# Three of four down batches in seven products, one operand sum made in DRAM by DMA, and activation sums three steps later, in a two-layer hybrid trunk

## The chip, the cores and the metric

The kernel runs on one core of one Trainium2 chip. The metric is device time in microseconds (us): the kernel before takes 2304.21 us, the median of three runs (2303.27 to 2304.63). All arithmetic that matters is fp32, done on TensorE as three products of split operands (below).

## The reference

Two layers over a sequence of 256 tokens and a width of 2048. Each layer is a mixer, a squared-ReLU MLP with a hidden width of 8192, and a gated embedding. Layer 0 mixes with differential attention, layer 1 with a gated recurrence.

```
for i in range(DEPTH):                       # DEPTH = 2
    xn = rmsnorm(h, g_mix[i])
    mix = diff_attention(...) if i % 2 == 0 else rglru_block(...)
    h = h + mix
    h = h + sqrelu_mlp(rmsnorm(h, g_mlp[i]), w_up[i], w_down[i])
    ple_gate = sigmoid(rmsnorm(h, g_ple[i]) @ w_ple_gate[i])
    h = h + ple_gate * (p[i] @ w_ple_proj[i])

def sqrelu_mlp(xn, w_up, w_down):            # w_up 2048x8192, w_down 8192x2048
    return square(relu(xn @ w_up)) @ w_down

def diff_attention(xn, w_qkv, ...):          # first of the program
    q, k, v = split(xn @ w_qkv); q = rmsnorm(q, g_q); k = rmsnorm(k, g_k); ...
```

## The kernel before, in words

Weights are streamed once from DRAM. SyncE's queue loads chunks of four 128-row tiles by 512 columns (1 MB) into a few raw buffers. `stream` walks over groups (one block of output columns each) and their steps; a step (`Sub`) is two weight tiles, 128x1024. For each step ScalarE writes a rounded copy `hi` (a cast) and VectorE the remainder `lo = raw - hi`; this pair of instructions is called a split here. TensorE then does three products for each pair of tiles: x_hi w_hi, x_lo w_hi, x_hi w_lo. Splits are written three steps ahead of the products, into four buffers in the attention part and six in the MLP.

The order of the work: the text is written step by step, `defer(n, ...)` puts a piece n steps later, and the framework's scheduler then lays out each engine's queue by its own estimate, letting an instruction go ahead of others on its engine when what it depends on is there. Each queue is then fixed, and an engine runs it strictly in order.

The q and k groups (eight, the first of the program): at the end of a group `qk_evict` takes 8 sums of squares (`q_ss`, VectorE), GpSimd makes `q_m` and `q_r` from them (`rstd`, L366 and L368), VectorE multiplies by `q_r` (L591) and goes on with the splits of the next group, which stand behind it in its queue.

The MLP: `up` groups (512 hidden columns each, 8 steps of 16 products) alternate with `down` groups. Two up groups make two batches of 512 hidden rows; a down group then multiplies up to four batches by 1024 of the 2048 output columns (one half). In a batch the product is a 2x2 block product; it is done plainly in 8 block products (4 steps of 12 matmuls), or by the Winograd form in 7 (7 steps of 6 matmuls). For a batch in seven, VectorE also makes sums of activation blocks (L810 to L815, at the end of the up group) and four sums of weight blocks (`split_form`, L470: U1 = W11 + W12, T2 = U1 + W22, T3 = W12 + W22, T4 = T2 + W21), and splits seven operands instead of four. Before the change, every second batch is in seven. `middle` and `evict` of `down` join the products and add them to the residual `h`.

The pool for 128x1024 sums and for the activation sums is `t4`, three buffers.

Of the kernel before, what the change touches and what calls it, by code (L numbers as in the profile page):

```python
# [9 lines left out]
F32 = mybir.dt.float32  # L10
# [51 lines left out]
class Group:  # L62
# [41 lines left out]
class Blocks:  # L104


    def __init__(self, w, b, n0):
        r0 = b * BT * P
        rows = w[r0 : r0 + BT * P].rearrange("(c p) n -> p c n", p=P)
        self.chunks = [Chunk(rows[:, :, n0 + i * NB : n0 + (i + 1) * NB], BT) for i in range(2)]  # L110
        for c in self.chunks:
            c.ring = 1
        self.sums = {}

    def of(self, name):
        if name in self.sums:
            return self.sums[name]
        return self.chunks[int(name[2]) - 1].raw[:, int(name[1]) - 1 :: 2]


class SevenGroup:
# [4 lines left out]
    def __init__(self, w, batches, n0, hid, middle, evict):  # L126
        self.hid, self.middle, self.evict, self.subs, self.pre = hid, middle, evict, [], {}
        self.what = []
        for b, seven in batches:
            bl = Blocks(w, b, n0)  # L130
            if seven:
                for i, (form, _, _) in enumerate(FORMS):
# [9 lines left out]
        self.first, self.last = {}, {}  # L142
        for i, (_, form, nj) in enumerate(self.what):
# [3 lines left out]
        self.mid = max(self.last[k] for k in ("P1", "P5", "P6", "P7"))  # L147
# [27 lines left out]
def trunk_kernel(ctx: ExitStack, tc, a, out):  # L175
# [24 lines left out]
    sm = ctx.enter_context(tc.tile_pool(name="sm", bufs=4))  # L200
    ps_acc = ctx.enter_context(tc.tile_pool(name="ps_acc", bufs=6, space=PSUM))
# [189 lines left out]
    class Norm(Wide):  # L391
# [35 lines left out]
        def feed(self, nb):  # L427
            self.stat(nb)
            for b in range(2):
                defer(1 + b, lambda b=b: self.transpose(nb, b))  # L430


    def stream(groups):
# [38 lines left out]

        def split_to(i):
            while done["split"] < min(i + 1, len(subs)):
# [22 lines left out]
        for g in groups:  # L497
# [6 lines left out]
            for i, s in enumerate(g.subs):  # L504
# [7 lines left out]
                if seven:  # L512
                    prods = g.products(i, s)
                    for q in prods:
                        if q[0] not in acc:
                            acc[q[0]] = ps_tp.tile([P, NB], F32, name="tp") if q[0] in ("P3", "Z") else psum([P, NB])
# [5 lines left out]
                    if i == g.mid:  # L522
                        g.middle(acc)
# [24 lines left out]
                run_due()  # L548
            g.evict(acc)
# [223 lines left out]
    SLOTS = 4  # L773

    def is_seven(b):
        return b % 2 == 0

    def mlp(l, norm_in, norm_out):
# [3 lines left out]
        def batch(b):  # L782

            if not is_seven(b):
                both = big([P, 2, 2, 4, P], F32R)
                return Batch(False, both[:, 0], both[:, 1])
            if "x" not in space:
                space["x"] = x32([P, 2, 2, 2, 7, P])
            both = space["x"][:, b % SLOTS // 2]
            return Batch(True, both[:, 0], both[:, 1])  # L790

        def up_evict(b):


            def evict(acc):
                hid[b] = bt = batch(b)
                for j in range(2):
# [3 lines left out]
                    for i in range(2):  # L801
# [4 lines left out]
                        nc.vector.tensor_tensor(halves[i], two(ps[:, :SEQ]), two(other), op=ALU.add)  # L806
                    nc.scalar.activation(x, x, AF.Relu)
# [18 lines left out]
        def down(half, bs):  # L826
# [3 lines left out]
            keep = {}  # L830

            def middle(acc):
                c1, cb = t4([P, 2, NB]), t4([P, 2, NB])
                keep["P1"], keep["M"], keep["B"], keep["N"] = c1[:, 0], c1[:, 1], cb[:, 0], cb[:, 1]
                nc.scalar.copy(keep["P1"], acc["P1"])
                nc.vector.tensor_tensor(keep["M"], keep["P1"], acc["P6"], op=ALU.subtract)
                nc.vector.tensor_tensor(keep["B"], acc["P7"], keep["M"], op=ALU.add)
                for k, o in (("M", "M"), ("N", "B")):
                    nc.vector.scalar_tensor_tensor(
                        keep[k], in0=acc["P5"], scalar=-1.0, in1=keep[o], op0=ALU.mult, op1=ALU.subtract  # L840
                    )

            def evict(acc):
                r2 = norm_in().r2
                for t, n, ps, other in ((0, 0, "P2", "P1"), (1, 0, "P4", "B"), (0, 1, "P3", "M"), (1, 1, "Z", "N")):
                    hb = h[:, t, hs[n]]
                    for part in (acc[ps], keep[other]):
                        nc.vector.scalar_tensor_tensor(
                            hb, in0=part, scalar=r2[:, t : t + 1], in1=hb, op0=ALU.mult, op1=ALU.add
                        )  # L850
# [4 lines left out]
            groups.append(SevenGroup(a["w_down"][l], [(b, is_seven(b)) for b in bs], n0, hid, middle, evict))  # L855

        for b in range(0, NBT, 2):
            up(b)
            up(b + 1)
            down(int(b % 4 == 0), range(max(b - 2, 0), b + 2))  # L860
        down(1, range(NBT - 2, NBT))


    def ple(l, norm_in, norm_out):
# [13 lines left out]
        def gate_evict(nb):  # L878
            def evict(acc):
# [5 lines left out]
                if nb == 3 and l == 0:  # L885
                    defer(8, lambda: p_setup(1))
# [248 lines left out]
    defer(40, lambda: p_setup(0))  # L1135
# [31 lines left out]
```

## Time and profile before

| | us |
|---|---|
| median of three runs | 2304.21 |
| the profiled execution: its own time | 2303.79 |
| its span, first to last instruction | 2301.9 |
| TensorE busy in the span | 2277.8 (99%) |
| VectorE busy | 1709.6 (74%) |
| ScalarE busy | 1355.5 (59%) |
| GpSimd busy | 47.3 (2%) |

432 MB come in by SyncE's queue, which keeps the 16 DMA engines busy for 55.5% of the span. The profiled execution stands 0.42 us under the median. Around its span lie 1.9 us. A matmul's shown duration is longer than its share of time, since matmuls overlap; the distance from one start to the next is what it costs. The same holds, less strongly, for VectorE's long instructions.

### The profile page before, as it was taken

What the parts mean: (1) busy time and instruction counts of PE and PEld (TensorE: products, weight loads), DVE (VectorE), ACT (ScalarE), POOL (GpSimd) and SP (SyncE); (2) the same over time, 40 slices, a digit from 0 to 9 for tenths busy, and PEclk for the clock granted to TensorE, in tenths of its full rate; (3) what the DMA queues carried; (4) which work ended last, traced back from release to release, by engine and by line L of the source; (5) the groups of instructions that cost most, each with busy time, mean ns of one, the idle gap of its engine ahead of it and who ended that gap; (6) DMA issues with size and microseconds to landing.
All of it is one profiled execution on the core that took longest, in us unless ns stands there. A gap on an engine that the chain in (4) does not pass through costs nothing. (4 is left out here: it accounts for less than half of the span.)

```text
span 2301.9 us, 29004 instructions
## 1 busy us (share of the span) xinstructions
PE 2277.8 (99%) x11275; PEld 1913.4 (83%) x11275; DVE 1709.6 (74%) x2048; ACT 1355.5 (59%) x1836; POOL 47.3 (2%) x79
## 2 busy tenths in 40 slices
PE   8999999999999999999999999999999999999999
PEld 7888888888888888887888887888888888888787
DVE  6676655778878868879666767568887887887974
ACT  6555555655655645646557887555564564564653
POOL 2100000000000000000000000000000000000000
PEclk9999999999999999999999999999999999999999
DMA  7455556456547547545555565645745645745464
GB/s 244 165 185 168 165 171 214 168 182 237 181 162 242 187 161 244 175 162 186 193 190 190 165 201 173 202 157 200 256 151 179 238 167 181 239 167 179 174 210 146
DMA packets 221050, 434.80 MB, mean 189 GB/s; under 512 B 7326, under 2 KB 12064, under 8 KB 220912
## 3 DMA queue, kind: packets, MB, share of 16 engines
q1 hardware_dynamic: 220256, 432.04, 55.5%
q8 instruction: 88, 1.44, 0.3%
q0 software_dynamic: 608, 0.89, 0.2%
q14 instruction: 50, 0.41, 0.1%
q10 hardware_dynamic: 48, 0.02, 0.0%
HBM read 430.82 MB, written 2.10 MB: 188 GB/s over the span
## 5 line engine op out<-in xcount | busy, mean ns | idle before, releaser
L357 DVE TENSOR_TENSOR w_lo<-w_raw,w_hi 128x1024 fp32r<-128x1024 f32 x465 | 564.2, 1221 | 304.5 <-ACT w_hi L356 304.4
L356 ACT CAST w_hi<-w_raw 128x1024 fp32r<-128x1024 f32 x465 | 486.6, 1051 | 419.4 <-PE acc L352 214.9
L537 PE MATMUL acc<-x,w_hi 128*128 128x512 f32 x1368 | 477.3, 396 | 0.0
L350 PE MATMUL acc<-w_hi,x 128*128 128x512 f32 x1152 | 457.1, 397 | 0.0
L351 PE MATMUL acc<-w_lo,x 128*128 128x512 f32 x1152 | 450.4, 391 | 1.9 <-DVE w_lo L357 1.9
L352 PE MATMUL acc<-w_hi,x 128*128 128x512 f32 x1152 | 450.6, 391 | 0.0
L537 PE MATMUL acc<-x,w_lo 128*128 128x256 f32 x1368 | 368.5, 279 | 0.0
L537 PEld LDWEIGHTS acc<-x,w_hi 128*128 128x128 f32 x1368 | 251.9, 188 | 54.7
L537 PEld LDWEIGHTS acc<-x,w_lo 128*128 128x128 f32 x1368 | 257.8, 188 | 7.4
L352 PEld LDWEIGHTS acc<-w_hi,x 128*128 128x128 f32 x1152 | 216.7, 188 | 46.7 <-DVE x L357 0.2
L351 PEld LDWEIGHTS acc<-w_lo,x 128*128 128x128 f32 x1152 | 217.2, 189 | 44.9 <-DVE w_lo L357 3.1
L350 PEld LDWEIGHTS acc<-w_hi,x 128*128 128x128 f32 x1152 | 216.8, 188 | 41.7
L464 ACT CAST w_hi<-t 128x1024 fp32r<-128x1024 f32 x85 | 89.2, 1051 | 128.8 <-PE acc L537 73.9
L537 PE MATMUL acc<-x,big 128*128 128x512 f32 (+1 forms) x688 | 127.7, 338 | 0.0
L356 ACT CAST w_hi<-big 128x1024 fp32r<-128x1024 f32 x87 | 90.7, 1050 | 62.6 <-PE acc L537 26.7
L471 DVE TENSOR_TENSOR w_lo<-t,w_hi 128x1024 fp32r<-128x1024 f32 x85 | 103.8, 1222 | 30.3 <-ACT w_hi L464 30.1
L537 PE MATMUL acc<-x,v 128*128 128x512 f32 (+1 forms) x672 | 124.8, 338 | 0.0
L537 PEld LDWEIGHTS acc<-x,big 128*128 128x128 f32 x688 | 107.9, 188 | 15.5
L537 PEld LDWEIGHTS acc<-x,v 128*128 128x128 f32 x672 | 105.9, 188 | 15.0
L357 DVE TENSOR_TENSOR w_lo<-big,w_hi 128x1024 fp32r<-128x1024 f32 x87 | 105.3, 1218 | 14.1 <-ACT w_hi L356 14.1
L471 DVE TENSOR_TENSOR w_lo<-w_raw,w_hi 128x1024 fp32r<-128x1024 f32 x64 | 78.0, 1219 | 31.9 <-ACT w_hi L464 31.9
L518 PE MATMUL acc<-w_hi,x 128*128 128x512 f32 x256 | 100.3, 392 | 1.4 <-ACT w_hi L464 1.3
(277 smaller groups left out, 3570.0 us busy)
## 6 DMA issues: line engine op xcount, KB each, us to landing
w_raw<-in_w_up_dram SPq DMA_DIRECT2D x96, 1024.0 KB, 5.5
w_raw<-in_w_down_dram SPq DMA_DIRECT2D x96, 1024.0 KB, 5.2
w_raw<-in_w_qkv_dram SPq DMA_DIRECT2D x47, 1024.0 KB, 5.1
big<-in_w_up_dram SPq DMA_DIRECT2D x32, 1024.0 KB, 5.6
big<-in_w_down_dram SPq DMA_DIRECT2D x32, 1024.0 KB, 7.3
w_raw<-in_w_ple_gate_dram SPq DMA_DIRECT2D x32, 1024.0 KB, 5.2
w_raw<-in_w_in_rec_dram SPq DMA_DIRECT2D x32, 1024.0 KB, 5.4
w_raw<-in_w_o_attn_dram SPq DMA_DIRECT2D x16, 1024.0 KB, 5.1
```

The lines of the kernel that those rows point to most:

```text
L350: nc.tensor.matmul(ps, lhsT=lh, rhs=rh, start=start, stop=False)
L351: nc.tensor.matmul(ps, lhsT=lh, rhs=rl, start=False, stop=False)
L352: nc.tensor.matmul(ps, lhsT=ll, rhs=rh, start=False, stop=stop)
L356: nc.scalar.copy(hi, src)
L357: nc.vector.tensor_tensor(lo, src, hi.bitcast(F32), op=ALU.subtract)
L464: nc.scalar.copy(s.hi, src)
L471: nc.vector.tensor_tensor(s.lo, src, s.hi.bitcast(F32), op=ALU.subtract)
L518: nc.tensor.matmul(acc[k], lhsT=lh, rhs=rh, start=first, stop=False)
L537: nc.tensor.matmul(o, lhsT=lh, rhs=rh, start=k == 0 and n == 0, stop=k == g.nk - 1 and n == 1)
```

## The change

1. `is_seven` becomes `b % 4 != 1`: of 16 batches of a half, 12 are in seven products and 4 plain (before 8 and 8). `batch` gets other buffers for this.
2. The seven operands come in another order (W11, W21, W22, U1, T2, T3, T4), and three sums are left on VectorE. The fourth, U1 = W11 + W12, is made in DRAM: `Blocks.prepare` copies 512 KB of W12 to a scratch tensor and adds 512 KB of W11 to it, by two DMAs of GpSimd's queue, the second an accumulating one that waits for the first. SyncE later loads the scratch tensor in place of W12. `prepare` is written into the steps of the two up groups ahead of the down group that uses it (`g.pre`).
3. The ReLU, the square and the activation sums of a batch come three steps after the end of its up group (`defer(3, finish)`).
4. The joining of the products (`done`) is done as each product's last step is past, not in the middle and at the end.
5. Two pieces of small work move: the transposes of the norm behind the MLP (`feed`) come later, and the preparation of `p` (`p_setup`) moves into the last down groups.

The sixth split buffer of the MLP is put into memory left over (`spare`, `wx`).

```
-    ("W11", X11, "P1"), ("U1", S1, "P5"), ("T2", S2, "P6"), ("T3", S3, "P7"), ("W21", X12, "P2"),
-    ("T4", X22, "P4"), ("W22", S4, "P3"),
+    ("W11", X11, "P1"), ("W21", X12, "P2"), ("W22", S4, "P3"), ("U1", S1, "P5"), ("T2", S2, "P6"),
+    ("T3", S3, "P7"), ("T4", X22, "P4"),
 )
-SUMS = {"U1": ("W11", "W12"), "T2": ("U1", "W22"), "T4": ("T2", "W21"), "T3": ("W12", "W22")}
+SUMS = {"T2": ("U1", "W22", ALU.add), "T3": ("T2", "W11", ALU.subtract), "T4": ("T2", "W21", ALU.add)}
...
+    def prepare(self, nc, scratch):
+
+        nc.gpsimd.dma_start(scratch, self.cols[1][:, 0::2])
+        nc.gpsimd.dma_start(scratch, self.cols[0][:, 0::2], accum_op=ALU.add)
+        dst, _ = self.chunks[1].pieces[0]
+        self.chunks[1].pieces[0] = (dst, scratch)
...
+    scratch = ctx.enter_context(tc.tile_pool(name="scratch", bufs=10, space=bass.MemoryType.DRAM))
...
             if after in SUMS:
-                load_to(cidx[id(bl.chunks[1])])
-                one, two = (bl.of(nm) for nm in SUMS[after])
+                one, two, op = SUMS[after]
                 bl.sums[after] = t4([P, SK, NB])
-                nc.vector.tensor_tensor(bl.sums[after], one, two, op=ALU.add)
+                nc.vector.tensor_tensor(bl.sums[after], bl.of(one), bl.of(two), op=op)
...
-                    if i == g.mid:
-                        g.middle(acc)
+                    for k in acc:
+                        if g.last[k] == i:
+                            g.done(k, acc)
...
     def is_seven(b):
-        return b % 2 == 0
+        return b % SLOTS != 1
...
+                    fs.append((j, f, x))
+
+                def finish():
+                    for e in fs:
+                        form(*e)
+
+                defer(3, finish)
...
-                        norm_out().feed(2 * half + n)
+                        norm_out().feed(2 * half + n, 2 + 2 * n if half else 4 + 3 * n)
+                    if half == 0:
+                        defer(7, lambda: p_setup(l))
...
+            todo = [bl for g in groups[at + 2 :] for bl in g.sevens]
+            for i, bl in enumerate(todo):
+                g = groups[at + i % 2]
+
+                def prepare(_, bl=bl):
+                    bl.prepare(nc, scratch.tile([P, SK, NB], F32, name="u1"))
+
+                g.pre[1 + 2 * (i // 2)] = prepare
```

How the change moves instructions, at the two places that matter.

First, GpSimd's queue in the q and k part, at the start of the program. Before the change, between `q_m` (L366) and `q_r` (L368) of a group and those of the next stands nothing, or one small load:

```order
L366 TENSOR_SCALAR q_m<-q_ss 128x8 [waits DVE_49]
L300 DMA t_426<-in_lam_k_dram 128x128 [waits DMASW5_49]
L368 TENSOR_TENSOR q_r<-q_m,mhalf 128x8 [waits Pool_49]
L366 TENSOR_SCALAR q_m<-q_ss 128x8 [waits DVE_49]
L368 TENSOR_TENSOR q_r<-q_m,mhalf 128x8 [waits Pool_49]
L366 TENSOR_SCALAR q_m<-q_ss 128x8 [waits DVE_49]
L368 TENSOR_TENSOR q_r<-q_m,mhalf 128x8 [waits Pool_49]
L366 TENSOR_SCALAR q_m<-q_ss 128x8 [waits DVE_49]
L368 TENSOR_TENSOR q_r<-q_m,mhalf 128x8 [waits Pool_49]
```

After the change the same queue, from the second `q_m` on (now L383, with `q_r` at L385; L124 is the copy of a block of W12 to a scratch tensor `u`, L125 the accumulating DMA onto it; DMASW are the counters of GpSimd's own DMAs):

```order
L383 TENSOR_SCALAR q_m<-q_ss 128x8 [waits DVE_49]
L124 DMA u_7188<-in_w_down_dram 256x1x512 [waits DMASW4_49]
L385 TENSOR_TENSOR q_r<-q_m,mhalf 128x8 [waits Pool_49]
L124 DMA u_7738<-in_w_down_dram 256x1x512 [waits DMASW5_49]
L124 DMA u_7783<-in_w_down_dram 256x1x512
L125 DMA u_7188<-in_w_down_dram 256x1x512 [waits DMASW4_49]
L125 DMA u_7738<-in_w_down_dram 256x1x512 [waits DMASW5_49]
L125 DMA u_7783<-in_w_down_dram 256x1x512 [waits DMASW6_49,DMASW1_49]
L124 DMA u_7929<-in_w_down_dram 256x1x512 [waits DMASW2_49]
L124 DMA u_8472<-in_w_down_dram 256x1x512 [waits DMASW3_49]
L124 DMA u_8517<-in_w_down_dram 256x1x512
L125 DMA u_7929<-in_w_down_dram 256x1x512 [waits DMASW2_49]
```

Eight more DMAs follow before the third `q_m`; before the change nothing stood between. All 96 DMAs of `prepare`, of both layers, stand in GpSimd's queue ahead of the seventh and eighth `q_m`: 16 ahead of the first `q_m` and, between one `q_m` and the next, 14, 18, 14, 17, 14 and 3. None stands in the MLP's part of the queue. The scratch tensors are 48 different ones, so that no copy waits for a reader.

Second, VectorE's queue at the end of the second up group of a pair (batches 6 and 7 of layer 0) and the start of the down group. Before (L806 joins the halves of the up products, L471 and L357 are splits, of a batch in seven and of a plain one; the 128x512 rows are batch 7's activations):

```order
L471 TENSOR_TENSOR w_lo_5802<-t4_5782,w_hi_5801 128x1024
L471 TENSOR_TENSOR w_lo_5849<-t4_5804,w_hi_5848 128x1024
L471 TENSOR_TENSOR w_lo_5862<-w_raw_5734,w_hi_5861 128x1024
L806 TENSOR_TENSOR t2_5824<-acc_5647,t1_5825 128x2x128
L806 TENSOR_TENSOR t2_5824<-acc_5648,t1_5828 128x256
L806 TENSOR_TENSOR t2_5835<-acc_5649,t1_5836 128x2x128
L806 TENSOR_TENSOR t2_5835<-acc_5650,t1_5839 128x256
L471 TENSOR_TENSOR w_lo_5875<-t4_5864,w_hi_5874 128x1024
L357 TENSOR_TENSOR big_5823<-t2_5824,big_5823 128x512
L357 TENSOR_TENSOR big_5823<-t2_5835,big_5823 128x512
L471 TENSOR_TENSOR v4_5886<-w_raw_5759,v4_5885 128x1024
```

After, at the same place (L833 joins the halves, L486 is a sum of weight blocks, L487 a split of a batch in seven, L846 to L851 the activation sums):

```order
L487 TENSOR_TENSOR w_lo_5895<-w_raw_5834,w_hi_5894 128x1024
L833 TENSOR_TENSOR t4_5878<-acc_5687,t1_5879 128x2x128
L833 TENSOR_TENSOR t4_5878<-acc_5688,t1_5882 128x256
L833 TENSOR_TENSOR t4_5885<-acc_5689,t1_5886 128x2x128
L486 TENSOR_TENSOR t4_5897<-w_raw_5834 128x1024
L833 TENSOR_TENSOR t4_5885<-acc_5690,t1_5889 128x256
L846 TENSOR_TENSOR t4_5878<-t4_5878 128x256
L850 TENSOR_TENSOR t4_5878<-t4_5878 128x128
L851 TENSOR_TENSOR t4_5878<-t4_5878 128x128
L487 TENSOR_TENSOR w_lo_5908<-t4_5897,w_hi_5907 128x1024
L374 TENSOR_TENSOR big_5877<-t4_5878,big_5876 128x896
L846 TENSOR_TENSOR t4_5885<-t4_5885 128x256
```

Before, five of the seven operands' splits and all four sums stand ahead of the join; after, four splits and no sum, and batch 7, now in seven too, puts six activation sums and two larger splits between the rest. In TensorE's queue the products of the plain batch are drawn forward between those of T3 and T4.

## Rows read from the trace of the kernel before

**Rows 1.** The page, part 1: busy time, share of the span, instructions.

```profile
PE 2277.8 (99%) x11275; PEld 1913.4 (83%) x11275; DVE 1709.6 (74%) x2048; ACT 1355.5 (59%) x1836; POOL 47.3 (2%) x79
```

**Rows 2.** Waits: engine, line, waited for: us in total, times, longest.

```profile
POOL q_m L366 <- DVE q_ss L586: 133.6, 7, 25.6
...
DVE t L591 <- POOL q_r L368: 14.7, 8, 2.0
...
PEld acc L518 <- ACT big L464: 7.3, 5, 1.8
```

**Rows 3.** Timeline of TensorE: start, us, instruction; last attention and first seven-product steps.

```profile
399.72 0.39 PE L350 MATMUL acc<-w_hi,x 128*128 128x512 f32 x1
...
402.44 0.86 PE L537 MATMUL acc<-x,big 128*128 128x512 f32 x4
...
448.08 0.40 PE L518 MATMUL acc<-w_hi,x 128*128 128x512 f32 x1
...
449.46 0.40 PE L518 MATMUL acc<-v,x 128*128 128x512 f32 x1
...
450.87 0.40 PE L518 MATMUL acc<-big,x 128*128 128x512 f32 x1
```

**Rows 4.** Windows of two up groups and their down group (busy us, clock, DMA).

```profile
468.67:513.66 44.99, 44.99 (x258) 39.15 (x256) 33.18 (x40) 22.08 (x29) 0.00 (x0) 1.00 0.43 145
513.66:554.68 41.02, 41.02 (x181) 33.77 (x180) 37.75 (x40) 27.97 (x32) 0.00 (x0) 1.00 0.76 260
```

**Rows 5.** Timeline of VectorE in that down group.

```profile
513.07 1.61 DVE L806 TENSOR_TENSOR t<-acc,t 128x256 f32<-128x256 f32 x4
516.94 1.29 DVE L357 TENSOR_TENSOR big<-t,big 128x512 fp32r<-128x512 f32 x2 [2.25 <-ACT big L356]
...
519.55 1.22 DVE L471 TENSOR_TENSOR w_lo<-w_raw,w_hi 128x1024 fp32r<-128x1024 f32 x1
520.69 2.35 DVE L357 TENSOR_TENSOR w_lo<-w_raw,w_hi 128x1024 fp32r<-128x1024 f32 x2
```

**Rows 6.** Instructions by line: VectorE's activation sums (busy us, mean ns).

```profile
L810 DVE TENSOR_TENSOR t<-t 128x256 f32<-128x256 f32 x32 | 12.7, 419 | 0.2
...
L814 DVE TENSOR_TENSOR t<-t 128x128 f32<-128x128 f32 x32 | 7.9, 284 | 0.0
```

**Rows 7.** Timeline of GpSimd in the q and k part.

```profile
9.13 0.62 POOL L319 TENSOR_SCALAR_AFFINE_SELECT mtab<-mtab 128x512 f32<-128x512 f32 x1
...
40.15 0.20 POOL L366 TENSOR_SCALAR q_m<-q_ss 128x8 f32<-128x8 f32 x1 [11.31 <-DVE sfc L342]
...
41.02 2.01 POOL L368 TENSOR_TENSOR q_r<-q_m,mhalf 128x8 f32<-128x8 f32 x1
...
132.67 0.80 POOL L559 DMA_DIRECT2D t<-in_p_dram  x1 [19.14 <-issue]
...
161.72 0.20 POOL L366 TENSOR_SCALAR q_m<-q_ss 128x8 f32<-128x8 f32 x1 [18.68 <-DVE q_ss L586]
```

**Rows 8.** Timeline of VectorE where it takes the first `q_r`.

```profile
43.07 1.23 DVE L591 TENSOR_TENSOR t<-t,q_r 128x1024 f32<-128x1024 f32 x1 [1.57 <-POOL q_r L368]
44.21 1.22 DVE L357 TENSOR_TENSOR w_lo<-w_raw,w_hi 128x1024 fp32r<-128x1024 f32 x1
```

**Rows 9.** Windows: the last two columns are the DMA engines' share and GB/s.

```profile
0.00:10.00 10.00, 2.48 (x9) 1.61 (x9) 2.78 (x5) 3.77 (x6) 7.17 (x19) 1.00 0.80 265
10.00:20.00 10.00, 9.85 (x37) 8.11 (x38) 6.29 (x8) 8.42 (x17) 0.00 (x0) 1.00 1.04 374
...
140.00:160.00 20.00, 19.55 (x95) 16.01 (x94) 12.91 (x15) 10.08 (x13) 2.75 (x2) 1.00 0.58 192
```

**Rows 10.** DMA issues: queue, KB each, median us from issue to landing.

```profile
w_raw<-in_w_ple_proj_dram SPq DMA_DIRECT2D x8, 512.0 KB, 3.7
...
out_dram<-h SPq DMA_DIRECT2D x8, 256.0 KB, 3.1
...
t<-in_p_dram POOLq DMA_DIRECT2D x2, 256.0 KB, 3.2
```

More of the change, by code (lines that the diff above doesn't have):

```diff
@@ L104, with __init__ @@
 class Blocks:
-    def __init__(self, w, b, n0):
+    def __init__(self, w, b, n0, seven):
         r0 = b * BT * P
         rows = w[r0 : r0 + BT * P].rearrange("(c p) n -> p c n", p=P)
-        self.chunks = [Chunk(rows[:, :, n0 + i * NB : n0 + (i + 1) * NB], BT) for i in range(2)]
-        for c in self.chunks:
+        cols = [rows[:, :, n0 + i * NB : n0 + (i + 1) * NB] for i in range(2)]
+        self.chunks = [Chunk(c, BT) for c in cols]
+        for i, c in enumerate(self.chunks):
             c.ring = 1
-        self.sums = {}
+            if seven:
+                half = lambda raw, i: raw[:, i * SK : (i + 1) * SK]
+                c.pieces = [(lambda raw, i=i: half(raw, i), cols[c is self.chunks[1]][:, i::2]) for i in range(2)]
+        self.sums, self.cols = {}, cols
+    def prepare(self, nc, scratch):
[3 more added lines that the diff above has]
+        self.chunks[1].pieces[0] = (dst, scratch)
     def of(self, name):
@@ L117, in of, with __init__ @@
             return self.sums[name]
-        return self.chunks[int(name[2]) - 1].raw[:, int(name[1]) - 1 :: 2]
+        n, k = {"W11": (0, 0), "W21": (0, 1), "U1": (1, 0), "W22": (1, 1)}[name]
+        return self.chunks[n].raw[:, k * SK : (k + 1) * SK]
 class SevenGroup:
     flip = False
-    def __init__(self, w, batches, n0, hid, middle, evict):
-        self.hid, self.middle, self.evict, self.subs, self.pre = hid, middle, evict, [], {}
-        self.what = []
+    def __init__(self, w, batches, n0, hid, done, evict):
+        self.hid, self.done, self.evict, self.subs, self.pre = hid, done, evict, [], {}
+        self.what, self.sevens = [], []
         for b, seven in batches:
-            bl = Blocks(w, b, n0)
+            bl = Blocks(w, b, n0, seven)
             if seven:
+                self.sevens.append(bl)
                 for i, (form, _, _) in enumerate(FORMS):
@@ L782, in batch @@
         def batch(b):
+            at = b % SLOTS
             if not is_seven(b):
@@ L843, in evict @@
-            def evict(acc):
[L844 to L850, printed above, removed]
+            keep, have = {}, set()
@@ new lines, in add, with done @@
+            def add(t, n, part):
+                hb = h[:, t, hs[n]]
+                nc.vector.scalar_tensor_tensor(
+                    hb, in0=part, scalar=norm_in().r2[:, t : t + 1], in1=hb, op0=ALU.mult, op1=ALU.add
+                )
+            def done(k, acc):
+                have.add(k)
+                if k in ALONE:
+                    add(*ALONE[k], acc[k])
+                if k == "P1":
+                    c1 = t4([P, 2, NB])
+                    keep["P1"], keep["M"] = c1[:, 0], c1[:, 1]
+                    nc.scalar.copy(keep["P1"], acc["P1"])
+                if "A" not in have and {"P1", "P6"} <= have:
+                    have.add("A")
+                    nc.vector.tensor_tensor(keep["M"], keep["P1"], acc["P6"], op=ALU.subtract)
+                if "B" not in have and {"A", "P7"} <= have:
+                    have.add("B")
+                    cb = t4([P, 2, NB])
+                    keep["B"], keep["N"] = cb[:, 0], cb[:, 1]
+                    nc.vector.tensor_tensor(keep["B"], acc["P7"], keep["M"], op=ALU.add)
+                if "M" not in have and {"B", "P5"} <= have:
+                    have.add("M")
+                    for q, o in (("M", "M"), ("N", "B")):
+                        nc.vector.scalar_tensor_tensor(
+                            keep[q], in0=acc["P5"], scalar=-1.0, in1=keep[o], op0=ALU.mult, op1=ALU.subtract
+                        )
@@ L857, in mlp @@
+            groups.append(SevenGroup(a["w_down"][l], [(b, is_seven(b)) for b in bs], n0, hid, done, evict))
         for b in range(0, NBT, 2):
+            at = len(groups)
             up(b)
@@ L860, in mlp @@
             down(int(b % 4 == 0), range(max(b - 2, 0), b + 2))
-        down(1, range(NBT - 2, NBT))
+            if b == NBT - 2:
+                down(1, range(NBT - 2, NBT))
+            if b == NBT - 2:
+                groups[-1].closing = True
+            todo = [bl for g in groups[at + 2 :] for bl in g.sevens]
[4 more added lines that the diff above has]
+                g.pre[1 + 2 * (i // 2)] = prepare
     def ple(l, norm_in, norm_out):
```

47 lines of the change are left out of this document (22 added, 25 removed).

## The prediction

> **What bounds the kernel now.** I read the page's busy shares first: TensorE is busy 99% of the span [rows 1], so the time is the sum of its instructions, and of the 24 us left 7.5 lie in the first 10 [rows 9]. The waits come second: those of TensorE's own rows for a split are some microseconds in the whole run [rows 2]. VectorE and ScalarE are slower in places but hidden by the buffers ahead of TensorE. Third, the windows of one MLP round: in the two up groups VectorE is busy 33.18 of 44.99 us, in the down group 37.75 of 41.02 [rows 4]. So the down groups are where VectorE has next to nothing left. Fourth, the timeline of GpSimd: it does almost nothing, but its `q_r` is waited for by VectorE eight times [rows 2], and behind that multiply stand the splits of the next group [rows 8]. It is a narrow bridge in the q and k part: what is late on GpSimd is late on VectorE, and after the few steps split ahead, on TensorE.
>
> **The products removed.** Batches in seven rise from 8 to 12 of 16 in each of two halves and two layers: 16 more. A batch in seven has 42 matmuls, a plain one 48, so 16 x 6 = 96 matmuls go. Six of them make one step: 449.46 - 448.08 = 1.38 us, and 450.87 - 449.46 = 1.41 [rows 3]; with 1.38 that is 22.1 us, all on TensorE, which sets the end. Nothing else of TensorE's work changes in number.
>
> **VectorE in the MLP.** Long instructions follow each other every 1.14 us (519.55 to 520.69 [rows 5]), though each is shown with 1.22. Of 128x1024 a batch in seven had 7 splits and 4 sums, now 7 and 3, since U1 comes from DRAM; a plain one has 4. A down group of four batches had 2 x 11 + 2 x 4 = 30 and has 3 x 10 + 4 = 34: 4 x 1.14 = 4.6 us more. Where the second up group makes a batch now in seven (b = 3 of 4; 4 down groups in each layer), its activation sums come in too: 2 x (0.42 + 0.28 + 0.28) [rows 6] (the third of these lines is like the second) and two larger splits, some 0.6 us: 2.6 us. So 37.75 becomes 44.9 us in 8 down groups and 42.3 in 6, and TensorE's part shrinks from 41.02 to 39.64. The overflow of 5.3 and 2.7 us must be done ahead, in the 11.8 us that VectorE idles in the up groups, or TensorE waits. Ahead there is room for six split buffers, as before. Three things soften it: the stall of 2.25 us for batch activations [rows 5] is filled now, since they come three steps later; TensorE's queue puts the plain batch's products between those of T3 and T4, which are late; and a plain batch (11 us of TensorE for 4 x 1.14 of VectorE) pays back 6 us wherever it stands. Followed down VectorE's queue, with 1.14 a piece and nothing idle, the group with batch 3 has its last T4 ready some 3 us late and the other one in time. 8 x 3 = 24, less what TensorE already loses there: I take +15 us. Bounds: 0, and nothing softened, 8 x 5.3 + 6 x 2.7 = 59. ScalarE has 13 us free in a down group [rows 4] and gets 3 casts more; the SyncE loads have the same bytes in smaller pieces. I cost both at nothing.
>
> **GpSimd and the DMAs.** This is the large term. The 96 DMAs of `prepare` depend on nothing but each other, and in GpSimd's queue they stand not in the up groups but in the q and k part, 93 of them (48 copies, 45 accumulating) ahead of the sixth `q_m`. That instruction runs at 161.72 us [rows 7]. An accumulating DMA waits on the queue for its copy's landing, so nearly all 93 must have moved before `q_m` can start, and TensorE's group behind it hangs on `q_r`. Issuing them is no matter: 0.80 us for the one like them [rows 7], 74 us in all, spread out.
>
> What a DRAM-to-DRAM copy costs no row shows. Bounds for 0.524 MB: the highest rate of any window is 374 GB/s at a DMA share of 1.04 [rows 9], that is 1.40 us with all 16 engines full; from above 3.7 us, the landing of a load of that size alone [rows 10], as if one went after another. For a copy that both reads and writes DRAM I take the middle between 1.40 and twice that, 2.1 us: a store of 256 KB lands in 3.1 us, about like GpSimd's load of that size, 3.2 [rows 10], so writing is no slower than reading, but both go to the same memory. For the accumulating one, which reads two operands and writes one, the middle between twice and three times 1.40: 3.5 us; from above twice 3.7 = 7.4.
>
> The weights need the same engines. Up to the sixth `q_m`, six groups of 4.19 MB, three chunks ahead (3.1) and x (2.1) are 30.4 MB, 81 us at 374 GB/s, of which the first 9 us move 265 GB/s x 9 = 2.4 MB, 6 us [rows 9]. The shares add up, since a window at 1.04 has nothing left. So, from the first copy at 9 us [rows 7]: 9 + 48 x 2.1 + 45 x 3.5 + 75 = 9 + 101 + 157 + 75 = 342 us, against 161.7: 180 us late. In every interval before it the DMAs (14 to 18 at 2.8 us on average, and 11 us of weights) take longer than the group's 22 to 28 us, so the lateness grows group by group, and only three DMAs are left after the sixth. Covered are three steps split ahead, 3 x (402.44 - 399.72) = 8 us [rows 3]. I take +172 us. From below: 93 x 1.40 + 75 + 9 = 214, 52 late, +44 us. From above: 48 x 3.7 + 45 x 7.4 + 9 = 520, with the weights in the gaps, 358 late, +350 us.
>
> The Trainium skill has a rule that speaks against this part (Collectives: The Full Stack, "The bandwidth ceiling: the fold count and why AG ≠ RS ≠ AR"): a reducing DMA moves about half of what a copying one does, since two source reads go through one ring. By it, with 2.1 for the copy, the accumulating one is 4.2 us, an estimate, and the sum is 45 x 0.7 = 31 us larger; no row here shows it. Another page (DMA: Bandwidth & Descriptors, "Latency and other measured facts") gives 214 GB/s as the full rate of copies between HBM tensors, 2.45 us for this size, an estimate too, which would add 48 x 0.35 = 17 us.
>
> **Sum.** 2303.8 (the profiled execution: span 2301.9 and 1.9 around it) - 22.1 + 15 + 172 = 2468.7 us; the median is 0.4 us higher, which I neglect: 2469. What hides the rest: the moved transposes and `p_setup` are a handful of instructions beside 40 us groups.
>
> **Rivals.**
>
> 1. The DMAs run beside the weights and delay nothing; the products removed are the whole of it. For it: the DMA engines are idle 42% of the q and k part (share 0.58 [rows 9]). Against it: 93 DMAs in the 153 us to 161.7, with the weights beside them, would need 93 x 0.524 + 28 = 77 MB, 500 GB/s, where the fullest window has 374. It decides from (161.7 + 8 + 22 - 9 - 75) / 93 = 1.16 us a DMA downward. Time: 2303.8 - 22.1 + 0 to 15 = 2282 to 2297, faster. Chance 0.07.
> 2. The DMAs move at the highest rate of a load and VectorE keeps up: 2303.8 - 22.1 + 44 = 2326, up to 2400 for rates between. For it: no row says that a copy costs an engine more than a load. Against it: it reads and writes the same memory. Still slower. Chance 0.16.
> 3. Queued one behind the other: each accumulating DMA waits for its copy, the pattern is three and three, and a landing takes 3 us even when little moves [rows 10]. 2303.8 - 22.1 + 350 + 0 to 59 = 2632 to 2691, from 2570 on counted here. Chance 0.13.
> 4. The queue that I read is not what decides, and the DMAs go in the up groups after all: there 3 pairs x 5.6 = 17 us fit into 45 x 0.57 = 26 us of free engines [rows 4], and the time is that of rival 1. Chance 0.01.
>
> **How the numbers follow.** My forecast, late by 110 to 270 us, has 0.63, with a range of its own of 2400 to 2570. For 8 in 10 the range goes from 2335 to 2640: it takes in most of rival 2, whose lower end needs both the peak rate throughout and no wait in the MLP, and half of rival 3. About 0.2% (4.6 us) is what a measurement of this kernel can tell from no change. Faster by more: rivals 1 and 4, 0.07, since 2297 at the worst is still 7 us under; within: 0.02; slower: the rest, 0.91.
>
> **What would show it.** In the profile after: GpSimd's `q_m` no longer at 22 to 28 us intervals but at 35 to 70, each released by a DMA and not by `q_ss`; VectorE waiting for `q_r` in the first 350 us by 150 us or more in total; TensorE's busy digits at 5 or 6 there, its clock granted lower in part of it, and DMA digits of 9. In the MLP no DMA on GpSimd's queue, down groups of about 40 to 43 us instead of 41 to 42.7, VectorE at over 95% in them. It is wrong if the eighth `q_m` runs before 230 us (rival 1), if copies land at 1.4 us apart (rival 2), or if the down groups take over 46 us (the bound on VectorE).

## The result and the profile after

The changed kernel takes 2448.19 us (median of 4 runs, 2446.84 to 2451.54), before it is 2304.34 us (2303.27 to 2304.63) in the same runs: a ratio of 1.0627, 95% interval 1.0609 to 1.0646. The profiled execution has a span of 2445.0 us, 143.1 more than before. The prediction was 2469 us, 2335 to 2640, slower. Time and mechanism came out, but two terms of the sum were off in opposite directions: the q and k part lost 52 us less than forecast, VectorE in the MLPs cost 31 us more, most of it at their ends, which the sum had not. That the time came within 1% is partly luck, since the two errors cancel to 22 us.

The page of the changed kernel, parts 1 and 2 (busy time; busy tenths in 40 slices of 61 us, the granted clock, the DMA engines' share):

```profile
PE 2295.0 (94%) x11179; PEld 1907.7 (78%) x11179; DVE 1800.2 (74%) x2158; ACT 1403.9 (57%) x1884; POOL 131.3 (5%) x175
...
PE   7665699999999999999999999999999999999999
...
PEclk9887899999999999999999999999999999999999
DMA  9999955655457555654455655656456456555444
```

TensorE has 96 instructions fewer than in [rows 1] and 94% in place of 99%. Most of what is missing lies in the first five slices, where the DMA engines are full. The windows there, one MLP round further on, and one at the end (length in us; busy us of PE, PEld, DVE, ACT, POOL; clock, DMA share, GB/s):

```profile
0.00:10.00 10.00, 2.48 (x9) 1.60 (x9) 2.78 (x5) 3.84 (x6) 7.70 (x21) 1.00 0.79 252
10.00:20.00 10.00, 9.18 (x34) 7.57 (x35) 4.77 (x6) 5.26 (x10) 4.42 (x6) 1.00 1.04 395
...
140.00:160.00 20.00, 5.06 (x15) 4.20 (x16) 4.62 (x5) 0.69 (x1) 7.13 (x8) 0.51 1.01 250
588.53:633.54 45.01, 45.01 (x258) 39.19 (x257) 30.01 (x38) 21.21 (x29) 0.00 (x0) 1.00 0.42 137
633.54:677.06 43.52, 40.85 (x174) 31.64 (x172) 42.52 (x46) 27.93 (x32) 0.00 (x0) 1.00 0.59 199
723.06:763.06 40.00, 40.00 (x175) 32.48 (x174) 39.40 (x42) 29.12 (x34) 0.00 (x0) 1.00 0.66 225
2261.73:2341.73 80.00, 70.14 (x285) 54.78 (x284) 77.93 (x88) 48.59 (x64) 0.80 (x1) 0.91 0.42 142
```

The window from 140 us answers to the last of [rows 9]: TensorE is busy 5.06 of 20 us in place of 19.55, at a granted clock of 0.51, near its lower level of 1.2 GHz, where it had 1.00. In the MLP the up groups last as long as in [rows 4]. The down group shown second, which follows batch 3, lasts 43.52 us with VectorE busy in 42.52 of them; groups of this kind reach the first products of the next up group after 38.7 to 43.5 us. The one shown without such a batch lasts 40.00. The last row is for the ends, below.

The waits (us in total, times, longest):

```profile
POOL u L125 <- DMA u<-in_w_down_dram: 171.5, 38, 12.2
...
DVE t L611 <- POOL q_r L385: 97.2, 8, 23.1
...
PE tp L624 <- DVE t L611: 93.9, 6, 19.8
```

The three rows are read as one chain, from top to bottom. GpSimd's accumulating DMAs (L125) wait on its queue for their copies; VectorE's multiply waits for `q_r` 97.2 us, 14.7 before [rows 2]; TensorE's transposes wait for that multiply. GpSimd's own timeline shows why `q_r` is late (start, us, instruction, in brackets the idle time before it and what ended it):

```profile
82.40 2.57 POOL L124 DMA_DIRECT2D u<-in_w_down_dram  x3
97.18 1.05 POOL L125 DMA_DIRECT2D u<-in_w_down_dram  x1 [12.21 <-DMA u<-in_w_down_dram]
99.17 1.04 POOL L125 DMA_DIRECT2D u<-in_w_down_dram  x1 [0.94 <-DMA u<-in_w_down_dram]
101.15 1.03 POOL L125 DMA_DIRECT2D u<-in_w_down_dram  x1 [0.94 <-DMA u<-in_w_down_dram]
102.25 0.20 POOL L383 TENSOR_SCALAR q_m<-q_ss 128x8 f32<-128x8 f32 x1
...
272.95 0.20 POOL L383 TENSOR_SCALAR q_m<-q_ss 128x8 f32<-128x8 f32 x1
281.08 1.10 POOL L125 DMA_DIRECT2D u<-in_w_down_dram  x1 [7.93 <-DMA u<-in_w_down_dram]
281.71 2.15 POOL L385 TENSOR_TENSOR q_r<-q_m,mhalf 128x8 f32<-128x8 f32 x1
...
330.39 0.20 POOL L383 TENSOR_SCALAR q_m<-q_ss 128x8 f32<-128x8 f32 x1 [18.77 <-DVE q_ss L606]
```

VectorE's timeline shows when the data of the second `q_m` was written:

```profile
86.95 0.69 DVE L606 TENSOR_REDUCE q_ss<-t 128x4 f32<-128x512 f32 x1 [0.47 <-ACT t L605]
```

Three copies are issued, then three accumulating DMAs, the first of which holds the queue for 12 us; `q_m` follows at 102.25 with nothing idle before it: its data had been there since 87.64. The sixth runs at 272.95 us, at 161.72 before [rows 7], and its `q_r` even waits for one more DMA between the two. The eighth is late by 330.39 - 210.81 = 119.6 us, and so is the first up group of the MLP (522.05 against 402.44).

Cut at the starts of the first up group and of the last two down groups of each layer, the 143.1 us are:

| stretch | before, us | after, us | difference |
|---|---|---|---|
| to the MLP of layer 0 | 402.44 | 522.05 | +119.61 |
| MLP 0 to the start of its last two down groups | 630.06 | 630.73 | +0.67 |
| from there to MLP 1 | 468.95 | 478.99 | +10.04 |
| MLP 1 to the start of its last two down groups | 629.72 | 629.96 | +0.24 |
| from there to the end | 170.73 | 183.27 | +12.54 |

### The profile page after: what moved, and what is told of

It reads as the page before. It is cut to its first block, busy times and chain, and to the rows that moved or that the text cites. A ratio compares the mean times of both kernels' runs of the same rounds, so it can differ in the third digit from the quotient of the medians.

```text
span 2445.0 us, 29214 instructions
## 1 busy us (share of the span) xinstructions
PE 2295.0 (94%) x11179; PEld 1907.7 (78%) x11179; DVE 1800.2 (74%) x2158; ACT 1403.9 (57%) x1884; POOL 131.3 (5%) x175
## 5 line engine op out<-in xcount | busy, mean ns | idle before, releaser
L374 DVE TENSOR_TENSOR w_lo<-w_raw,w_hi 128x1024 fp32r<-128x1024 f32 x448 | 543.8, 1222 | 301.8 <-ACT w_hi L373 301.2
L373 ACT CAST w_hi<-w_raw 128x1024 fp32r<-128x1024 f32 x448 | 465.2, 1050 | 391.7 <-PE acc L369 212.8
L554 PE MATMUL acc<-x,w_hi 128*128 128x512 f32 x1400 | 488.3, 396 | 2.3 <-ACT w_hi L373 2.3
L367 PE MATMUL acc<-w_hi,x 128*128 128x512 f32 x1152 | 462.7, 403 | 3.0 <-ACT x L377 3.0
L368 PE MATMUL acc<-w_lo,x 128*128 128x512 f32 x1152 | 455.6, 396 | 5.1 <-DVE w_lo L374 5.1
L369 PE MATMUL acc<-w_hi,x 128*128 128x512 f32 x1152 | 455.7, 396 | 1.1 <-DVE x L378 1.1
L368 PEld LDWEIGHTS acc<-w_lo,x 128*128 128x128 f32 x1152 | 220.3, 191 | 49.8 <-DVE w_lo L374 7.1
L487 DVE TENSOR_TENSOR w_lo<-w_raw,w_hi 128x1024 fp32r<-128x1024 f32 x108 | 130.0, 1220 | 40.8 <-ACT w_hi L481 40.8
L481 ACT CAST w_hi<-w_raw 128x1024 fp32r<-128x1024 f32 x108 | 111.4, 1049 | 72.3 <-PE acc L554 64.7
L481 ACT CAST w_hi<-t 128x1024 fp32r<-128x1024 f32 x94 | 97.9, 1048 | 59.8 <-DVE t L486 45.4
L487 DVE TENSOR_TENSOR w_lo<-t,w_hi 128x1024 fp32r<-128x1024 f32 x94 | 114.6, 1219 | 10.6 <-ACT w_hi L481 10.3
L486 DVE TENSOR_TENSOR t<-t,w_raw 128x1024 f32<-128x1024 f32 x96 | 116.8, 1218 | 0.2
L554 PE MATMUL acc<-x,x 128*128 128x512 f32 x312 | 110.3, 395 | 0.0
L624 PE MATMUL tp<-ident,t 128*128 128x128 f32 x64 | 12.5, 330 | 93.9 <-DVE t L611 93.9
L534 PE MATMUL acc<-w_hi,big 128*128 128x512 f32 x236 | 93.1, 394 | 1.5 <-ACT w_hi L481 1.5
```

Of the source, the lines that this page charges most:

```text
L367: nc.tensor.matmul(ps, lhsT=lh, rhs=rh, start=start, stop=False)
L368: nc.tensor.matmul(ps, lhsT=lh, rhs=rl, start=False, stop=False)
L369: nc.tensor.matmul(ps, lhsT=ll, rhs=rh, start=False, stop=stop)
L373: nc.scalar.copy(hi, src)
L374: nc.vector.tensor_tensor(lo, src, hi.bitcast(F32), op=ALU.subtract)
L486: nc.vector.tensor_tensor(bl.sums[after], bl.of(one), bl.of(two), op=op)
```

## Experiments

The first four take the change apart: the place of the DMAs, GpSimd's part in the loss, the DMAs left out, and the DMAs alone. Before stood at 2303.48 us in these runs.

**e1_held**: each copy waits for the up matmul of its step.

```
+        copy = nc.gpsimd.dma_start(scratch, self.cols[1][:, 0::2])
+        tc.add_manual_dep(
+            copy.ins, mm.ins.name, mybir.DependencyInfo(mybir.DependencyClass.Sync, mybir.DependencyReason.DATA),
...
         nc.gpsimd.dma_start(scratch, self.cols[0][:, 0::2], accum_op=ALU.add)
```

> After, but each copy of `prepare` waits for the up matmul of its step, so that the 96 DMAs stand in the up groups of GpSimd's queue and not in the q and k part. Theory (GpSimd's queue holds q_m back; that is +119.6 us; the other +23.5 us are VectorE's, in the last down groups): the sixth q_m is back at 162 +- 3 us, the MLP of layer 0 starts at 402 +- 4, the time is 2448.2 - 119.6 = 2329 us, 2320 to 2340. Rival (it is the traffic that costs, wherever it stands): an up group shows a DMA share near 1 and lasts 2 to 4 us longer, some 16 x 3 = 48 us, and the time is 2365 to 2390.

Measured: 2328.37 us, 1.0111 (1.0096 to 1.0126). The sixth `q_m` runs at 159.64 us, the MLP starts at 400.37. An up group and the down group behind it:

```profile
466.84:511.85 45.01, 45.01 (x258) 39.20 (x256) 30.01 (x38) 21.20 (x29) 5.18 (x6) 1.00 0.73 207
511.85:555.35 43.50, 40.85 (x174) 31.68 (x172) 42.51 (x46) 27.91 (x32) 0.00 (x0) 1.00 0.61 199
```

The up group now has six DMAs on GpSimd and a DMA share of 0.73 in place of 0.42, and lasts the same 45.01 us. The same transfers that cost 119.8 us (2448.19 - 2328.37) in the q and k part are nearly free here: from the start of each MLP to its last two down groups, e1 takes 631.20 and 633.24 us, after 630.73 and 629.96, together 3.8 us more. The rival falls.

**e2_rstd_dve**: the DMAs stay in the q and k part; `rstd`, which waits behind them on GpSimd, goes to VectorE. A reciprocal stands in for the power, and the square root is left out.

```
-        nc.gpsimd.tensor_scalar(m, ss, 1.0 / width, EPS, op0=ALU.mult, op1=ALU.add)
-        nc.gpsimd.tensor_tensor(r, m, mhalf[:, :n], op=ALU.pow)
+        nc.vector.tensor_scalar(m, ss, 1.0 / width, EPS, op0=ALU.mult, op1=ALU.add)
+        nc.vector.reciprocal(r, m)
...
-                nc.gpsimd.tensor_tensor(self.r2, self.r, self.r, op=ALU.mult)
+                nc.vector.tensor_tensor(self.r2, self.r, self.r, op=ALU.mult)
```

> After, with all 96 DMAs where they are, but rstd (q_m, q_r and their like) on VectorE, with a reciprocal in place of the power -0.5 (the square root is left out, so the output is not the reference's). Theory in its strict form (the queue alone): the q and k groups return to 22 to 28 us, the MLP of layer 0 starts at 402 to 415, 2329 to 2342 us. Rival (traffic alone: the DMA engines are full, the weights come late whatever waits on GpSimd): the MLP still starts at 510 to 530, 2435 to 2455. Between (both): if the weights get half of the 280 GB/s that the full engines move, a group of 4.19 MB takes 30 us in place of 25, +40 to +64 us, 2370 to 2395.

Measured: 2377.91 us, 1.0332 (1.0315 to 1.0349); the MLP starts at 454.11. So of the 119.6 us, 522.05 - 454.11 = 67.9 go when `rstd` leaves GpSimd's queue, and 454.11 - 402.44 = 51.7 stay. Neither strict theory holds; the time lies in the range of the middle one. Windows and waits of this run:

```profile
40.00:80.00 40.00, 26.08 (x106) 20.97 (x105) 18.25 (x44) 12.45 (x18) 12.54 (x16) 0.79 1.06 276
80.00:120.00 40.00, 37.40 (x173) 30.69 (x173) 25.93 (x46) 20.79 (x38) 10.83 (x14) 0.96 1.06 315
120.00:160.00 40.00, 37.90 (x180) 31.03 (x179) 21.45 (x25) 17.07 (x21) 11.21 (x13) 1.00 1.06 318
...
280.00:320.00 40.00, 38.83 (x195) 32.38 (x194) 27.18 (x52) 22.16 (x46) 11.19 (x13) 1.00 1.06 312
```

```profile
POOL u L125 <- DMA u<-in_w_down_dram: 222.5, 47, 13.6
...
ACT w_hi L373 <- DMA w_raw<-in_w_qkv_dram: 109.4, 32, 5.8
```

GpSimd waits for its copies even longer than in after, but no instruction waits for GpSimd's arithmetic any more. From 80 us on TensorE is back at 37 to 39 of 40 us, and ScalarE's casts wait 109.4 us for the weights `w_qkv`.

The window from 40 us is another matter. The small loads of `lam_q` and `lam_k` (L317) still stand in GpSimd's queue behind the DMAs (the timelines of GpSimd, VectorE and TensorE):

```profile
56.11 1.18 POOL L317 DMA_DIRECT2D t<-in_lam_k_dram  x1
...
71.56 0.43 DVE L321 TENSOR_TENSOR t<-t 128x256 f32<-128x256 f32 x1 [17.63 <-DMA t<-in_lam_k_dram]
...
73.65 0.80 PE L368 MATMUL acc<-w_lo,x 128*128 128x512 f32 x1 [13.92 <-DVE w_lo L374]
```

Before, the last of these loads is issued at 40.41 us and VectorE does not wait for it. Here it is issued 15.7 us later and lands some 15 us after its issue; VectorE waits 17.63 us for it and TensorE 13.92 for the split behind. So the 51.7 us are not the traffic alone: about 14 of them hang on a load that the DMAs hold up in the queue and on its way. For the traffic beside the weights some 38 us are left, an estimate by difference, so the middle theory's range came true and its reason only in part.

**e3_no_dma**: U1 on VectorE again, no scratch.

```
-SUMS = {"T2": ("U1", "W22", ALU.add), ...
+SUMS = {"U1": ("W11", "W12", ALU.add), "T2": ("U1", "W22", ALU.add), ...
...
-                g.pre[1 + 2 * (i // 2)] = prepare
+                pass
```

> After, without the DMAs: U1 = W11 + W12 is made on VectorE again, 48 sums of 128x1024, and no DRAM scratch. Theory: the q and k part is as before (MLP of layer 0 at 402 +- 4), and VectorE has 3 sums more in a down group of four batches that it already fills to 98%: 14 x 3 x 1.14 = 48 us at most, so 2329 + 20 to 48 = 2349 to 2377 us. Rival (VectorE's idle 15 us in the up groups take them up): 2329 +- 6, the DMAs buy nothing at all.

Measured: 2364.11 us, 1.0267 (1.0252 to 1.0283), 35.7 us over e1: the DMAs do buy something, most of the 48 us that were expected at most. The same down group as the second row of e1:

```profile
512.23:558.80 46.57, 42.04 (x174) 33.05 (x172) 45.10 (x48) 28.09 (x32) 0.00 (x0) 0.96 0.56 186
```

VectorE's 45.10 us set its 46.57.

**e4_before_dmas**: the kernel before with the 96 DMAs and nothing else.

```
...
+                    bl.prepare(nc, scratch.tile([P, SK, NB], F32, name="u1"))
...
```

> Before, with nothing of the change but its 96 DMAs into the DRAM scratch, which nothing reads. In GpSimd's queue they stand among the q_m as in after (16 ahead of the first, 93 ahead of the sixth). Theory: the q and k part loses what it loses in after, the MLP of layer 0 starts at 522 +- 8, the MLP and the end are as before: 2304.3 + 119.6 = 2424 us, 2414 to 2434. Rival (part of the loss comes from the loads of the scratch or from VectorE's other order): MLP at 480 or earlier, under 2400.

Measured: 2424.09 us, 1.0524 (1.0508 to 1.054); the MLP starts at 521.94, in after at 522.05. The loss in the q and k part belongs to the DMAs, wholly. The waits are those of after:

```profile
POOL u L119 <- DMA u<-in_w_down_dram: 171.6, 38, 12.3
...
DVE t L599 <- POOL q_r L376: 101.9, 8, 22.3
```

The second four ask for the price of accumulating and for the 22.5 us at the ends of the MLPs. Before: 2303.66 us.

**e5_second_copy**: the accumulating DMA made a copy, so that U1 is W11 alone.

```
-        nc.gpsimd.dma_start(scratch, self.cols[0][:, 0::2], accum_op=ALU.add)
+        nc.gpsimd.dma_start(scratch, self.cols[0][:, 0::2])
```

> After, with the accumulating DMA of each pair made a plain copy of the same bytes onto the same scratch (so U1 is W11 alone, and the output is not the reference's); as many DMAs, in the same places of GpSimd's queue, each second one still waiting for the first to land. Theory (a DMA that accumulates costs the engines no more than a copy; the queue's waits and the bytes do it): as after, 2448 us, 2440 to 2455, MLP of layer 0 at 522 +- 6. Rival (the prediction's price, 3.5 us against 2.1 for a copy): 48 x 1.4 = 67 us of engine time less, the MLP starts at 450 to 480, 2380 to 2410.

Measured: 2393.06 us, 1.0389 (1.0374 to 1.0405): 55.1 us under after. My theory falls, the prediction's difference between the two kinds was the better one. The sixth `q_m`, with the same 93 DMAs ahead of it, and a window:

```profile
225.75 0.20 POOL L383 TENSOR_SCALAR q_m<-q_ss 128x8 f32<-128x8 f32 x1
```

```profile
120.00:160.00 40.00, 24.75 (x104) 20.17 (x104) 14.59 (x15) 11.90 (x15) 15.67 (x22) 0.83 0.97 335
```

TensorE is busy in 24.75 of these 40 us, in after in 20.49.

The price of each kind can be read from GpSimd's DMA queue (q0: packets, MB, and the time of the packets as a share of 16 engines' span), here in before, after and e5:

```profile
q0 software_dynamic: 608, 0.89, 0.2%
...
q0 software_dynamic: 20576, 51.23, 8.8%
...
q0 software_dynamic: 14432, 51.23, 5.9%
```

The small loads of before take 0.2% of 2301.9 = 4.6 us. In e5, 5.9% of 2394.1 less these is 136.7 us for 96 copies, 1.42 us each. In after, 8.8% of 2445.0 less these is 210.6 us; 48 copies at 1.42 leave 142.4 for the 48 accumulating DMAs, 2.97 us each, 2.1 times a copy.

**e6_held_tail**: e1 with the last batch plain, and so without 8 of the 96 DMAs.

```
-        return b % SLOTS != 1
+        return b % SLOTS != 1 and b != NBT - 1
```

> e1_held with the last batch (b = 15) plain, so that the last down groups of each layer hold the batches in seven that they held before (12 and 14): 24 products more, 5.5 us. Theory (the last two down groups of a layer have no up group after them in which VectorE catches up: 3 x 10 + 4 and 2 x 10 long VectorE instructions, 54 x 1.14 = 62 us, and 16 us of sums onto h, against 59 us of products): the stretches behind the last up group fall back from 480.9 and some 183 us to 469 and 171 +- 2, the time to 2328.4 - 24 = 2304, 2300 to 2310. Rival (the later transposes, p_setup and the order of sums onto h are what costs there): the stretches stay, and the time rises by the products to 2332 to 2336.

Measured: 2309.06 us, 1.0023 (1.0014 to 1.0033), 19.3 us under e1 although 24 products more. The first stretch behind the last up group takes 468.82 us (480.88 in e1), the second 2308.1 - 2135.47 = 172.6 (180.5). The first 80 us of the second, to be read against the last row of the windows of after:

```profile
2135.47:2215.47 80.00, 77.31 (x348) 61.99 (x347) 70.38 (x84) 50.44 (x75) 1.85 (x4) 1.00 0.45 154
```

VectorE falls from 77.93 to 70.38 of 80 us, TensorE rises from 70.14 to 77.31, and its clock stays at 1.00. What is left, 5 us over before, lies mostly in the two stretches ahead of the last down groups (632.3 and 632.8 us, before 630.1 and 629.7), although 72 products fewer than before are 16.6 us. After, whose DMAs are not in the MLP, takes 630.73 and 629.96 there, so the held DMAs may be a part of it; that was not tried.

**e7_held_old_feed**: e1 with the norm's transposes fed as before the change.

```
-                        norm_out().feed(2 * half + n, 2 + 2 * n if half else 4 + 3 * n)
+                        norm_out().feed(2 * half + n)
```

> e1_held with the norm's transposes fed after 1 and 2 steps, as before the change, in place of 2 to 8 steps. Theory (VectorE's long instructions set the end of the MLP, the feeding does not): 2328 +- 6. Rival of e6_held_tail (the late feeding holds up the next part): 2328.4 - 12 to 24 = 2304 to 2316.

Measured: 2329.74 us, 1.0111 (1.0094 to 1.0128): as e1. The later feeding costs and gives nothing that can be measured.

**e8_gpsimd_u1**: e3 with the 48 sums of U1 on GpSimd.

```
+                on = nc.gpsimd if after == "U1" else nc.vector
+                on.tensor_tensor(bl.sums[after], bl.of(one), bl.of(two), op=op)
```

> e3_no_dma with the 48 sums U1 = W11 + W12 on GpSimd, which is idle in the MLP, in place of VectorE or DMAs. If a sum there takes under about 4 us (a form of a batch lasts 1.4 us on TensorE, and four of them are ahead) and takes nothing from VectorE: as e1_held, 2328 us, 2320 to 2335. If GpSimd and VectorE slow each other (long VectorE instructions over 1.3 us in the down groups): between e1_held and e3_no_dma (2364.1) or above it.

Measured: 2404.23 us, 1.0435 (1.0420 to 1.0451), 40 us above e3, on the rival's side. The sums on GpSimd, then splits and sums on VectorE from 600 to 1100 us (the number behind the comma is the mean ns of one), and the waits for GpSimd's sums:

```profile
L487 POOL TENSOR_TENSOR t<-w_raw 128x1024 f32<-128x1024 f32 x32 | 142.6, 4456 | 1047.1 <-DMA w_raw<-in_w_down_dram 668.1 <-DVE t L834 91.1 <-DVE w_lo L374 73.3
...
L374 DVE TENSOR_TENSOR w_lo<-w_raw,w_hi 128x1024 fp32r<-128x1024 f32 x48 | 64.1, 1351 | 20.6 <-ACT w_hi L373 20.4
...
L487 DVE TENSOR_TENSOR t<-t,w_raw 128x1024 f32<-128x1024 f32 x44 | 53.7, 1219 | 11.6 <-POOL t L487 11.4
```

```profile
ACT w_hi L481 <- POOL t L487: 91.6, 18, 5.9
```

A sum of 128x1024 takes 4.46 us on GpSimd and 1.22 on VectorE, and the cast of U1 waits for it. VectorE's splits stretch to 1.33 to 1.37 us in several groups of instructions. How much of the 40 us is the waits and how much the slower splits was not separated.

The last two tried to beat the kernel before (2303.24 us in these runs) from e6, by taking small sums off VectorE.

**e9_sums_gpsimd**:

```
-                        nc.vector.tensor_tensor(
+                        nc.gpsimd.tensor_tensor(
                             f[:, S3 : S1 + 1], f[:, X11 : X22 + 1 : X22 - X11],
... (and the sums of S2 and S4)
```

> e6_held_tail with the three sums of a batch's activations (128x256 and twice 128x128, two halves) on GpSimd in place of VectorE. They take 2.0 us of VectorE at the head of a down group, where TensorE stands for 1 to 3 us in every second group. Theory (VectorE is what a down group with the batch b = 3 of 4 lacks; in GpSimd's e8 rate, 4.46 us for 128x1024, the sums take 1.1 + 0.6 + 0.6 us a half, and stay small enough not to slow VectorE): 6 such groups a layer lose 1 to 2.6 us less, 2309.1 - 8 to 18 = 2291 to 2301 us, faster than before the change. Rival (GpSimd's queue or the slower VectorE, 1.33 in place of 1.22 us beside a GpSimd sum, eats it): 2305 to 2313.

**e10_sums_adds_gpsimd**: e9, and

```
+                        nc.gpsimd.tensor_scalar(
+                            keep[q], keep[q], norm_in().r2[:, at[0] : at[0] + 1], None, op0=ALU.mult
+                        )
+                        nc.gpsimd.tensor_tensor(hb, hb, keep[q], op=ALU.add)
```

> e9 and, in all down groups but the last ones, the sum of r2 x P1 onto h on GpSimd too, as a multiply in place and a sum of 128x512 (one VectorE instruction of 0.75 us less in a down group; some 4.5 us on GpSimd). Theory: another 0.5 us in each of the groups that VectorE sets, 2 to 6 us under e9. Rival: the slot of P1 is held longer, and the sums of the next group wait for it, or VectorE is slowed by 4.5 x 9% = 0.4 us in each: as e9 +- 2, or above.

Measured: 2325.81 us, 1.0098 (1.0081 to 1.0115), and 2325.82 us, 1.0097 (1.0082 to 1.0112). Both are 17 us worse than e6, so e9 lies above both of its expectations, and the second edit does nothing. The sums are short on GpSimd (a line of e9):

```profile
L850 POOL TENSOR_TENSOR t<-t 128x256 f32<-128x256 f32 x12 | 9.5, 834 | 36.1 <-ACT t L848 36.1
```

yet the down groups with batch 3 got longer: 42 to 47 us to the first products of the next up group in place of 39 to 43.5, and VectorE is idle in up to 5.6 us of one (46.65 us, busy 41.02). The steps of a batch (sums on GpSimd, cast, split) now cross engines more often, and their slot, of which there are three, is shared with the sums T2 to T4; that the slot is what holds them was not tried. GpSimd's queue is not: in these groups no DMA stands in it, and its sums wait for ScalarE. No run is faster than the kernel before.

## Why the prediction was right, and where its sum was not

**Products removed, -22.1 us.** Right: 96 instructions fewer, and in every down group that VectorE doesn't set the 174 products take 40.0 us for 41.0 [rows 4].

**VectorE in the MLP, +15 us.** Mis-sized, because it was counted for 14 down groups that are all followed by an up group. In the stretch ahead of a layer's last two down groups, 6 groups have 6 products fewer, 8.3 us, and yet it grew by 0.67 and 0.24: lost are 9.0 + 8.5 = 17.5 us. That is the term as meant. Not in the sum were the ends: in the last two down groups of each layer five of six batches are in seven products, and no up group follows, in whose idle VectorE time the arrears could be done. The 54 long VectorE instructions (34 + 20) at 1.14 us are 62 us, the sums onto h some 16, beside 59 us of products. These stretches should have become 2.76 us shorter each (12 products) and became 10.04 and 12.54 longer: 28.1 us lost. e6 shows it: with the old mix of batches there, VectorE has room again and the two stretches come back to within 2 us of before; e7 excludes the moved transposes, and e6 keeps the moved `p_setup` and the new order of the sums onto h, so these are not it either. So +45.6 in place of +15, within the bounds of 0 to 59, but not for the reason that made the bounds.

**GpSimd and the DMAs, +172 us.** The mechanism was right in each link (queue, `q_m`, `q_r`, VectorE, TensorE) and e4 shows it alone, e1 by taking it away. One link was missed: the load of `lam_k` behind the DMAs, seen in e2 (in after VectorE waits 8.5 us for it). The size was 52 too large: the DMAs were priced at 2.1 and 3.5 us, and took 1.42 and 2.97 of the engines' time (e5). The copy is thus near its lower bound, 1.40, a load at the fullest window's rate. With the measured prices the sum gives 9 + 48 x 1.42 + 45 x 2.97 + 75 = 286 us for the sixth `q_m`, and it ran at 272.95, 111 late. The 13 us between are about what the six DMAs cost that were issued in the last 8 us before it (3 x 1.42 + 3 x 2.97), and these need not have landed: for one of the copies the next accumulating DMA waits until 281.08. Two smaller things were off as well. One more accumulating DMA stood between `q_m` and `q_r` and held it for 8 us, so that `q_r` was late by 281.71 - 162.00 = 119.7; and of the cover of 8 us nothing was there: seventh and eighth `q_m` and the MLP are late by the same 119.6.

By the Trainium skill (Collectives: The Full Stack, "The bandwidth ceiling: the fold count and why AG ≠ RS ≠ AR") a reducing DMA moves about half of what a copy does. Here the accumulating DMA took 2.1 times a copy's engine time (2.97 for 1.42 us), so the trace agrees. The rate of another page of the Trainium skill (DMA: Bandwidth & Descriptors, "Latency and other measured facts"), which it gives for copies of other shapes from other queues, makes 2.45 us of this size as an estimate; the trace does not agree, with 1.42 us.

**The additive model** was right for the kernel as it is. With `q_m` on the queue, each group must wait for the DMAs ahead of it, and weights and DMAs add up. Without `rstd` in the queue it would have been wrong: in e2 the DMAs run on beside the weights at a share of 1.06 up to 320 us, and the loss is 51.7.

**The rivals.** Hidden (rival 1) and held in the up groups (4) did not happen; e1 is what 4 would have been, and even that is slower than before, since the ends cost more than the products bring: its 2282 to 2297 was wrong by 31 us. Rival 2's price for a copy came true (1.42 for 1.40), that for the accumulating DMA did not, and the time is 48 us above its range. Rival 3, each transfer by itself, is excluded by the copies that end GpSimd's idle times 2 us apart (97.18 to 101.15 us), and by the sixth `q_m` at 272.95 us, where it had 520.

**What would show it.** The first five `q_m` intervals were 36.6 to 48.6 us, as said (35 to 70), and the waits for `q_ss` came only with the seventh and eighth. VectorE's waits for `q_r` were 97.2 us, not 150 or more, which fits the smaller prices. Digits, clock and DMA share came as said; so did the down groups ahead of the ends, 38.7 to 43.5 us to the first products of the next up group. Of the signs of being wrong none came: the eighth `q_m` ran at 330.39 us, the copies ended the idle times shown 2 us apart, and no down group took 46 us there.

Open: what the lower granted clock adds in the q and k part (0.51 in the window shown) and at the ends (0.91). TensorE waits there anyway, and no run has the waits without the clock.

## What to carry to other kernels

An instruction that depends on nothing may be laid far ahead in its queue, here 93 of 96 DMAs ahead of the sixth `q_m`, and the queue is worked off in order: look at what short, needed work stands behind it, small loads included, not at where the code calls it. Tied to its step, the same traffic was nearly free (3.8 us). Where a second engine is within a few per cent of the bound, count its work to the end of the stage: with no lighter group behind, arrears that elsewhere are made up become time. And taking work off an engine isn't a gain in itself: the same sum was 3.7 times as long on GpSimd, and small sums moved there cost 17 us.

## What the runs showed of the hardware that was not expected

- Copies from DRAM to DRAM, 0.524 MB each, took 1.42 us of all the DMA engines' time (e5). By the same measure a load of that size took 1.55 (55.5% of 2301.9 us for 432 MB, before). One that accumulates took 2.97 us (after).
- Weights and DMAs share full engines (share 1.06 at 315 GB/s in e2), and from 80 us on the weights keep enough for TensorE to be busy 37 to 39 of 40 us.
- Six DRAM-to-DRAM transfers beside an up group (share 0.73 in place of 0.42, e1) left its time at 45.01 us.
- A sum of 128x1024 in f32: 4.46 us on GpSimd, 1.22 on VectorE (e8).
